# Second FFN product and output projection on 512 columns with four banks of their own, in a hybrid RWKV-7 / S5 block

## The chip, the cores and the metric

The kernel runs on one core of one Trainium2 chip. It is written in a tile language whose scheduler sets the order of the instructions on each engine by a simulated timeline; on the chip each engine then runs its own queue in that order. The metric is the device time of one launch in microseconds.

## What is computed

One layer of a diffusion backbone (2048 latent tokens and 256 context tokens of width 1024, all float32). The reference, cut to what matters:

```python
z = split(modulate(rmsnorm(x, norm1_g), mod[0], mod[1]) @ w_in)      # rwkv columns, gates, S5 columns
rwkv_x = rwkv_mixer(z[:8])    # 3x3 conv, bidirectional delta-rule scan, 8 heads x 64, head norm, gate
s5_x   = s5_mixer(z[8])       # bidirectional diagonal complex scan, 32 groups x 16, then GLU
x = x + mod[2] * (concat([rwkv_x, s5_x]) @ w_out)                    # output projection
h = modulate(rmsnorm(x, norm2_g), mod[3], mod[4])
x = x + mod[5] * ((silu(h @ ffn_w1) * (h @ ffn_w3)) @ ffn_w2)        # ffn_w2: the second FFN product
out = rmsnorm(x, final_g)
```

`modulate(h, shift, scale)` is `h * (1 + scale) + shift`, and the six `mod` vectors come from a small product of the conditioning vector with `mod_w`. The inner FFN width is 2816.

## The kernel before

**Products.** Each large product is made of three matmuls in reduced float32: both operands are split into a high and a low part (`split`: a copy on ScalarE gives the high part, a subtraction on VectorE the low part), and high x high, high x low and low x high are summed in PSUM. PSUM has eight banks of 128 partitions x 512 float32.

**Stages.** `Front` makes the mod vectors, norms and projects the tokens block by block (`project`, L222) and runs the convolutions, in one `f` bank and others of its own. The S5 stage (`s5_pairs`, matmuls L689 to L759, with 32 `mod_group`s beside it) uses three `f` banks of a pool `sf`. The RWKV scan is cut into 36 units of 128 tokens (`R.unit(h)`), which run all through Front, the S5 stage and the start of the last stage. A unit inverts a triangular matrix: 31 serial steps (L999 and L1001, on POOL for most units, on DVE for every second one in the S5 stage), transposes (L1004 to L1008), and two sets of small matmuls (L1014, L1021) that are copied out by ScalarE. Then `chain` runs twice (two chunks of 64 tokens), each a string of small matmuls and copies: L1047, L1052, L1061, L1068 and L1070 on DVE, L1074, L1076, L1082. Heads come in pairs: `par` 0 and 1 are the two halves of the partitions. Matmuls of `par` 0 write to a bank `p0`, those of `par` 1 to a bank `p1`; other banks of this part are `c` and `w`.

**Last stage** (class `Tail`). Four blocks of 512 tokens, in the order 3, 2, 1, 0. For each: `glu` (L1189), `readout` of RWKV (L1209 to L1259), `outproj` (a call of `product`), `norm` (L1340 on POOL makes four scaled identities, L1347 are its 32 matmuls), `ffn` in six parts of 4, 4, 4, 4, 4 and 2 row blocks (w1 and w3 at L1371, 512 tokens at a time; then `product` with w2), and `final`. Block 3's readout, projection, norm and first three FFN parts run beside the last twelve RWKV units and use a pool `fp` of three `f` banks. When the units are done, their pools close, `f2` and a PSUM pool `fq` of three `f` banks open in their place, and `aside(f2, fq)` makes `readout` and `norm` use those; FFN and `product` stay on the three banks of `fp`. From there the loop over b = 3, 2, 1 runs block b's FFN parts between the readout, projection and norm of block b − 1:

```python
early = T.ffn(b, SPLITS[3:5])
for _ in T.readout(b - 1, T.keep):
    next(early, None)
run(early)
T.outproj(b - 1, range(8))
T.norm(b - 1)
run(T.ffn(b, SPLITS[5:]))
```

**`product`** (L1295 to L1303) goes over four column blocks of 256. For each it holds two f banks (two tiles of 128 tokens in each), loads and splits one 128x256 block of weights per row block, runs 4 x 3 matmuls of 256 columns, multiplies by the gate on DVE (L1300, one bank at a time) and adds to the residual on POOL (L1303). On the last call for a block, `square` (L1311, ScalarE) sums the squares for the next norm.

Of the kernel before, what the change touches and what calls it, by code (L numbers as in the profile page):

```python
# [9 lines left out]
F32 = mybir.dt.float32  # L10
F32R = mybir.dt.float32r
# [71 lines left out]

def mod_group(tc, I, K, S, wt, st, fp, n, tag="f"):

    nc = tc.nc
    sec, part = divmod(n, 8)
    mw = I["mod_w"][0].rearrange("(k p) c -> p k c", p=P)
    pm = fp.tile([P, 512], F32, name=tag, bufs=2 if tag == "pa" else None)
# [9 lines left out]
    pc = fp.tile([P, 512], F32, name="f")  # L99
# [20 lines left out]
class Front:  # L120
# [36 lines left out]
    def mods(self):  # L157
        for n in range(16):
            mod_group(self.tc, self.I, self.K, self.S, self.xtile, lambda: self.stile()[:, 0:2 * P], self.fp, n, "pa")
        mod_vectors(self.tc, self.K, 0, (0, 2), "norm1_g", 0)  # L160
        mod_vectors(self.tc, self.K, 0, (1, 3), "norm1_g", 1)
# [621 lines left out]
class Rwkv:  # L783
# [200 lines left out]
    def inverse(self, h, dve):  # L984
# [21 lines left out]
        for q in range(4):  # L1006
            o = 32 * (q % 2)
            nc.vector.transpose(TW[32 * q:32 * q + 32, :, o:o + 32], TN[32 * q:32 * q + 32])  # L1008
        pz = [self.ph.tile([P, 2, 8, 32], F32, name="p%d" % par) for par in range(2)]
        Z = r.tile([P, 8, 32], F32, name="T2")  # L1010
        for b in range(8):
            for par in range(2):
                r0 = 64 * par
                mm(pz[par][r0 + 32:r0 + 64, 0, b, :], AX[1][r0:r0 + 32, :, b], TN[r0:r0 + 32, b, :], start=True, stop=True)  # L1014
        for par in range(2):
            r0 = 64 * par
            act(Z[r0 + 32:r0 + 64], pz[par][r0 + 32:r0 + 64, 0], AF.Copy)
        for b in range(8):
            for par in range(2):
                r0 = 64 * par  # L1020
                mm(pz[par][r0:r0 + 32, 1, b, :], Z[r0 + 32:r0 + 64, b, :], TW[r0 + 32:r0 + 64, b, 32:64], start=True, stop=True)  # L1021
        for par in range(2):
            r0 = 64 * par
            act(TW[r0:r0 + 32, :, 32:64], pz[par][r0:r0 + 32, 1], AF.Copy)

# [10 lines left out]
    def chain(self, h, cc):  # L1036
# [12 lines left out]
        act(R, rs, AF.Copy)  # L1049
        pp = [self.ph.tile([P, 2, 4, 64], F32, name="p%d" % par) for par in range(2)]  # L1050
        for hp, par in every:
            mm(pp[par][RH[par], 0, hp, :], TW[RH[par], cc * 4 + hp, :], R[RH[par], hp, :], start=True, stop=True)  # L1052
        for par in range(2):
            act(UV[RH[par], par], pp[par][RH[par], 0], AF.Copy, scale=-0.5)
        if not last:
# [16 lines left out]
        if h >= 2:  # L1072
            for hp, par in every:
                mm(pp[par][RH[par], 1, hp, :], UV[:, par, hp, :], AR[:, hp, par, :], start=hp == 0, stop=False)  # L1074
            for hp, par in every:
                mm(pp[par][RH[par], 1, hp, :], SV[RH[par], par, hp, :], Q[RH[par], hp, cc, 2, :],  # L1076
                   start=False, stop=hp == 3)
            if cc == 0:
                self.yw = r.tile([P, 4, 128], F32, name="YW")
            cs = slice(64 * cc, 64 * cc + 64)  # L1080
            for par in range(2):
                act(self.yw[RH[par], :, cs], pp[par][RH[par], 1], AF.Copy)  # L1082
# [26 lines left out]
class Tail:  # L1109


    def __init__(self, tc, I, K, S, out, f1, fp):
        self.tc, self.nc, self.I, self.K, self.S, self.out = tc, tc.nc, I, K, S, out
        self.f1, self.fp = f1, fp
        self.side = (f1, fp, "t", "s", "gh", "gl")
        self.C, self.H, self.X = {}, {}, {}
        nc, blk, ident = self.nc, K["blk"], K["ident"]
# [81 lines left out]
    def readout(self, b, put):  # L1199
# [26 lines left out]
        for hf in range(2):  # L1226
# [7 lines left out]
            for hp in range(4):  # L1234
# [175 lines left out]
def hybrid_block(tc, I, out):  # L1410
    with tc.tile_pool(name="dram", bufs=1, space=bass.MemoryType.DRAM) as dp, \
# [4 lines left out]
        with tc.tile_pool(name="a", bufs=1, side="right") as p, \  # L1416
# [11 lines left out]
            for bi in range(5):  # L1428
                if bi < 4:
                    A.block(bi, A.norm(bi + 1))  # L1430
                else:
# [85 lines left out]
```

## Time and profile before

| | us |
|---|---|
| median of 3 runs | 3798.66 |
| lowest and highest run | 3795.69, 3803.98 |
| the profiled execution, its own time | 3793.19 |
| span of its instructions | 3791.4 |

All rows of the trace come from this one profiled execution. Times in them are counted from the start of its span. In the lists of windows, the busy times stand in the order PE (TensorE matmul), PEld (its weight load), DVE (VectorE), ACT (ScalarE), POOL (GpSimd), each followed by its number of instructions. In a timeline a row can stand for several like instructions (x4), and the bracket names the idle time before it and what ended it. A matmul's own length includes its way through the array; the distance of two starts is what it costs when it follows another. Float32 matmuls that are not in the reduced form (those of L755 and L1014, for example) appear as two instructions each.

### The profile page before, as it was taken

Reading aid. Unit: us, or ns where it says so; the run is one execution under the profiler, and the core shown is the slowest. Engines: PE = TensorE matmul, PEld = TensorE weight load, DVE = VectorE, ACT = ScalarE, POOL = GpSimd, SP = SyncE. Lnnn points to the kernel's source line nnn. Section 1 sums busy time; section 2 is a strip of 40 time slices with the busy share of each in tenths; the row PEclk is TensorE's granted clock in tenths of the full one; section 3 lists DMA queues with packets and bytes.
Section 4 is the critical chain, followed back from the end, with each engine's and each line's share of the span. In section 5 each row is a group of like instructions: output and inputs, shape, how many; then the busy total and the mean of one; then the engine's idle time right before and its main releaser. Section 6 shows DMA issues by size and latency. Waiting matters only on the chain. (4 is left out here: it accounts for less than half of the span.)

```text
span 3791.4 us, 70356 instructions
## 1 busy us (share of the span) xinstructions
PE 3375.1 (89%) x25311; PEld 2815.1 (74%) x25311; DVE 2478.8 (65%) x4726; ACT 1710.7 (45%) x3777; POOL 1834.4 (48%) x3184
## 2 busy tenths in 40 slices
PE   5788887888867877889899999999999999999998
PEld 3666666666656666676777888988889888998887
DVE  7768776776778978856766656576444854454444
ACT  3565655645444343354555544454333533343333
POOL 3456667676767666566766662323212321231212
PEclk9798988898767887778889999999999999999999
DMA  6654544454234443276533334454333533333333
GB/s 184 192 138 106 153 120 131 131 141 119 85 105 115 132 142 104 75 168 143 129 90 99 105 98 149 123 164 130 102 98 103 178 101 101 106 100 120 103 100 94
DMA packets 789020, 462.34 MB, mean 122 GB/s; under 512 B 182544, under 2 KB 766868, under 8 KB 788672
## 3 DMA queue, kind: packets, MB, share of 16 engines
q1 hardware_dynamic: 788672, 457.85, 43.5%
q8 instruction: 200, 3.28, 0.4%
q14 instruction: 148, 1.21, 0.1%
HBM read 382.34 MB, written 75.36 MB: 121 GB/s over the span
## 5 line engine op out<-in xcount | busy, mean ns | idle before, releaser
L1303 POOL TENSOR_TENSOR X<-X,t 128x256 f32<-128x256 f32 x464 | 378.1, 842 | 937.3 <-DVE t L1300 936.6
L999 POOL TENSOR_TENSOR tmp<-AT,T 128x60 f32<-128x60 f32 (+24 forms) x992 | 401.2, 404 | 218.6 <-DVE AT L992 109.7
L1144 DVE TENSOR_TENSOR wl<-wr,wh 128x512 fp32r<-128x512 f32 x368 | 264.1, 719 | 312.8 <-PE f L1371 290.2
L1001 POOL TENSOR_TENSOR T<-T,tmp 128x60 f32<-128x60 f32 (+24 forms) x992 | 421.8, 425 | 66.7
L1143 ACT ACTIVATE wh<-wr 128x512 fp32r<-128x512 f32 x368 | 231.9, 631 | 439.9 <-PE f L1371 391.6
L1144 DVE TENSOR_TENSOR vl<-vr,vh 128x256 fp32r<-128x256 f32 x480 | 257.5, 538 | 262.6 <-ACT vh L1143 262.1
L1296 PE MATMUL f<-vl,gh 128*128 128x256 f32 x1408 | 397.2, 289 | 7.7 <-DVE vl L1144 7.5
L1371 PE MATMUL f<-H,wh 128*128 128x512 f32 x1408 | 389.0, 397 | 5.1 <-ACT wh L1143 3.8
L1297 PE MATMUL f<-vh,gl 128*128 128x256 f32 x1408 | 389.9, 284 | 0.0
L1371 PE MATMUL f<-L,wh 128*128 128x512 f32 x1408 | 388.6, 394 | 0.0
L1143 ACT ACTIVATE vh<-vr 128x256 fp32r<-128x256 f32 x480 | 199.2, 416 | 416.4 <-PE f L1297 360.9
L1371 PE MATMUL f<-H,wl 128*128 128x512 f32 x1408 | 386.1, 395 | 0.9 <-DVE wl L1144 0.9
L1295 PE MATMUL f<-vh,gh 128*128 128x256 f32 x1408 | 370.1, 287 | 3.7 <-ACT vh L1143 2.8
L255 DVE SCALAR_TENSOR_TENSOR acc<-zb,cw,acc 128x512 f32<-128x512 f32 (+2 forms) x384 | 307.0, 820 | 23.2 <-ACT acc L251 18.6
L1371 PEld LDWEIGHTS f<-L,wh 128*128 128x128 f32 x1408 | 262.9, 188 | 58.8
L1371 PEld LDWEIGHTS f<-H,wl 128*128 128x128 f32 x1408 | 261.9, 188 | 59.4 <-DVE wl L1144 1.4
L1371 PEld LDWEIGHTS f<-H,wh 128*128 128x128 f32 x1408 | 257.9, 189 | 59.2 <-ACT wh L1143 4.4
L1296 PEld LDWEIGHTS f<-vl,gh 128*128 128x128 f32 x1408 | 269.4, 191 | 18.6 <-DVE vl L1144 12.4
L1297 PEld LDWEIGHTS f<-vh,gl 128*128 128x128 f32 x1408 | 269.6, 192 | 1.2
L1295 PEld LDWEIGHTS f<-vh,gh 128*128 128x128 f32 x1408 | 256.1, 192 | 11.1 <-ACT vh L1143 4.5
L222 PE MATMUL pa<-HI,wl 128*128 128x512 f32 (+1 forms) x712 | 204.8, 407 | 41.4 <-POOL wl L219 30.0
L222 PE MATMUL pa<-HI,wh 128*128 128x512 f32 (+1 forms) x712 | 217.0, 426 | 20.0 <-ACT wh L218 9.7
(458 smaller groups left out, 7501.6 us busy)
## 6 DMA issues: line engine op xcount, KB each, us to landing
wr<-in_ffn_w_dram SPq DMA_DIRECT2D x352, 256.0 KB
raw<-in_w_in_dram SPq DMA_DIRECT2D x178, 256.0 KB
vr<-in_ffn_w_dram SPq DMA_DIRECT2D x352, 128.0 KB
ld<-s_rkvk SPq DMA_DIRECT2D x36, 768.0 KB
mraw<-in_mod_w_dram SPq DMA_DIRECT2D x64, 256.0 KB
vr<-in_w_out_dram SPq DMA_DIRECT2D x128, 128.0 KB
gq<-s_gate SPq DMA_DIRECT2D x116, 128.0 KB
SV<-s_vt SPq DMA_DIRECT2D x144, 64.0 KB
```

Of the source, the lines that this page charges most:

```text
L222: nc.tensor.matmul(pa[:, :nt], w[:, kc, :], h[:, 4 * kh + kc, :nt], start=kh + i + kc == 0, stop=kh == 1 and i == 2 and kc == 3)
L255: nc.vector.scalar_tensor_tensor(ag, zb[:, i0 - 1 + a:i0 - 1 + a + nr, e:e + 64], tap(a, e), ag, op0=OP.mult, op1=OP.add)
L999: eng.tensor_tensor(tv, AT[:, l + 1:, l:l + 1].to_broadcast([P, n, m]), T[:, l:l + 1, 0:m].to_broadcast([P, n, m]), op=OP.mult)
L1001: eng.tensor_tensor(T[:, l + 1:, 0:m], T[:, l + 1:, 0:m], tv, op=OP.add)
L1143: self.nc.scalar.activation(hi, x, AF.Copy)
L1144: self.nc.vector.tensor_tensor(lo, x, hi.bitcast(F32), op=OP.subtract)
L1295: mm(o, ah[:, js], vh, start=k == 0 and j % 2 == 0, stop=False)
L1296: mm(o, ah[:, js], vl, start=False, stop=False)
L1297: mm(o, al[:, js], vh, start=False, stop=k == n - 1 and j % 2 == 1)
L1303: nc.gpsimd.tensor_tensor(x, x, t[:, j], op=OP.add)
L1371: mm(p, a[:, kc, :], h[:, 4 * kh + kc, :], start=kh + i + kc == 0, stop=kh == 1 and i == 2 and kc == 3)
```

## The change

- In the RWKV part, the two tiles `p0` and `p1` become one tile `p`: the two halves of the partitions write to one bank, in the inverse (Z and its follower) and in the chain (U at index 0, y at index 1).
- The bank that this frees goes to `f`: two banks in place of one in `Front`, four in place of three in `sf` and in `fp`.
- When the units are done, a PSUM pool `fo` of four banks `o0` to `o3` opens in place of `fq`. `aside(f2, fo)` leaves `readout` and `norm` on the `f` banks of `fp`, which they now share with FFN's w1 and w3.
- `product` hands over to a new function `wide` once `fo` is set (that is, for all but block 3's projection and its FFN parts [:3]): two column blocks of 512, one bank for each of the four tiles of 128 tokens, weights loaded and split 128x512 at a time in `f2`, DVE's multiply and POOL's add on 128x512. `square` follows with 512 columns.
- The first block's `block(...)` call loses an empty S5 generator.

```diff
-        pz = [self.ph.tile([P, 2, 8, 32], F32, name="p%d" % par) for par in range(2)]
+        pz = self.ph.tile([P, 2, 8, 32], F32, name="p")
...
-                mm(pz[par][r0 + 32:r0 + 64, 0, b, :], AX[1][r0:r0 + 32, :, b], TN[r0:r0 + 32, b, :], start=True, stop=True)
+                mm(pz[r0 + 32:r0 + 64, 0, b, :], AX[1][r0:r0 + 32, :, b], TN[r0:r0 + 32, b, :], start=True, stop=True)
...
-        pp = [self.ph.tile([P, 2, 4, 64], F32, name="p%d" % par) for par in range(2)]
+        pp = self.ph.tile([P, 2, 4, 64], F32, name="p")
...
-        return self.fp.tile([P, 512], F32, name="f")
+        return self.fp.tile([P, 512], F32, name="f", bufs=2)
...
+        self.fo = None
...
-    def aside(self, f2, fq):
+    def aside(self, f2, fo):
-        self.side = (f2, fq, "nt", "ns", "zh", "zl")
+        self.side = (f2, self.fp, "nt", "ns", "zh", "zl")
+        self.fo = fo
...
+    def wide(self, b, A, n, wsrc, grow, last):
+        nc, f1, f2 = self.nc, self.f1, self.side[0]
+        mm = nc.tensor.matmul
+        X1 = self.X[b]
+        for cq in range(2):
+            cols = slice(512 * cq, 512 * cq + 512)
+            gq = f2.tile([P, 512], F32, name="gw", bufs=2)
+            nc.sync.dma_start(gq, bcast_row(grow[cols], 512))
+            po = [self.fo.tile([P, 512], F32, name="o%d" % j) for j in range(4)]
+            for k in range(n):
+                with self.tc.high_priority(offset=1000):
+                    raw = f2.tile([P, 512], F32, name="wr", bufs=3)
+                    nc.sync.dma_start(raw, wsrc(k, cols))
+                    vh = f2.tile([P, 512], F32R, name="wh", bufs=2)
+                    vl = f2.tile([P, 512], F32R, name="wl", bufs=2)
+                    self.split(vh, vl, raw)
+                ah, al = A[k]
+                for j in range(4):
+                    js = slice(j * P, (j + 1) * P)
+                    mm(po[j], ah[:, js], vh, start=k == 0, stop=False)
+                    mm(po[j], ah[:, js], vl, start=False, stop=False)
+                    mm(po[j], al[:, js], vh, start=False, stop=k == n - 1)
+            for j in range(4):
+                t = f1.tile([P, 512], F32, name="t", bufs=2)
+                nc.vector.tensor_tensor(t, po[j], gq, op=OP.mult)
+                x = X1[j][:, cols]
+                nc.gpsimd.tensor_tensor(x, x, t, op=OP.add)
+                if last:
+                    self.square(b, j, cq, t, 512)
...
     def product(self, b, A, n, wsrc, grow, last):
+        if self.fo:
+            return self.wide(b, A, n, wsrc, grow, last)
...
-             tc.tile_pool(name="sf", bufs=3, space=PSUM, side="right") as sf:
+             tc.tile_pool(name="sf", bufs=4, space=PSUM, side="right") as sf:
...
-        with tc.tile_pool(name="f1", bufs=1, side="right") as f1, tc.tile_pool(name="fp", bufs=3, space=PSUM, side="right") as fp:
+        with tc.tile_pool(name="f1", bufs=1, side="right") as f1, tc.tile_pool(name="fp", bufs=4, space=PSUM, side="right") as fp:
...
-            with tc.tile_pool(name="f2", bufs=1) as f2, tc.tile_pool(name="fq", bufs=3, space=PSUM) as fq:
-                T.aside(f2, fq)
+            with tc.tile_pool(name="f2", bufs=1) as f2, tc.tile_pool(name="fo", bufs=1, space=PSUM) as fo:
+                T.aside(f2, fo)
```

Since the scheduler decides, the change also moves instructions that it doesn't name. In the new kernel line numbers after L1113 are higher: FFN's L1371 is L1406, the norm's L1347 is L1382, glu's L1189 is L1191, `wide`'s matmuls are L1295 to L1297, and the old product's are L1330 to L1332. Three places on PE:

**Between the output projection and the norm of block 2** (o_… and f are PSUM banks, `nt` the scaled identity, X the residual rows). Before, with FFN matmuls and those of FFN's product in between:

```order
L1371 MATMUL f<-H,wl 128x512 x4
L1295 MATMUL f<-vh,gh 128x256
L1296 MATMUL f<-vl_27459,gh 128x256
L1297 MATMUL f<-vh,gl 128x256
L1371 MATMUL f<-H,wh 128x512 x4
L1371 MATMUL f<-L,wh 128x512 x4
L1371 MATMUL f<-H,wl 128x512 x4
L1295 MATMUL f<-vh,gh 128x256
L1296 MATMUL f<-vl_27459,gh 128x256
L1347 MATMUL f<-nt,X_26547 128x128
```

Now:

```order
L1296 MATMUL o_26305<-wl,H 128x512
L1297 MATMUL o_26305<-wh,L 128x512
L1296 MATMUL o_26306<-wl,H 128x512
L1297 MATMUL o_26306<-wh,L 128x512
L1296 MATMUL o_26307<-wl,H 128x512
L1297 MATMUL o_26307<-wh,L 128x512
L1382 MATMUL f<-nt,X_26127 128x128 x4
L1382 MATMUL f<-nt,X_26129 128x128 x4
```

The projection's last matmuls (whose weights-side operand is H or L, the split inputs of the projection) now stand right ahead of the norm's, and FFN's L1406 come behind all 32 of these. Blocks 1 and 0 read alike.

**Around the last RWKV unit** (TW and T are the inverse, UV and SV the chain's operands). Before, with FFN matmuls between the unit's groups:

```order
L1371 MATMUL f<-L,wh 128x512 x3
L1371 MATMUL f<-H,wl 128x512 x4
L1371 MATMUL f<-H,wh 128x512 x4
L1371 MATMUL f<-L,wh 128x512 x4
L1371 MATMUL f<-H,wl 128x512 x4
L1052 MATMUL p_22686<-R,TW_1085 64x64 x2
L1052 MATMUL p_22687<-R,TW_1085 64x64 x2
```

Now, the end of the unit before and the start of the last:

```order
L1061 MATMUL c<-UV,BT 64x64 x8
L1074 MATMUL p<-AR,UV 64x64 x8
L1076 MATMUL p<-Q,SV 64x64 x8
L1047 MATMUL c<-SV,Q 64x64 x8
L1014 MATMUL p<-tmp,AY 32x32 x16
L1021 MATMUL p<-TW_1085,T_22529 32x32 x16
L1052 MATMUL p<-R,TW_1085 64x64 x8
```

From the L1014 of the last unit but one to the first readout matmul of block 2, no FFN or product matmul stands in PE's queue. Earlier in this stage the fillers stand some tens of matmuls further ahead of the units than before.

**The end of the S5 matmuls** (L755 and L759). Before, behind the first matmuls of the 23rd unit's chain:

```order
L1061 MATMUL c<-UV,BT 64x64 x2
L759 MATMUL f<-ST,CQ 128x128
L755 MATMUL f<-U,TP 128x128 x2
L759 MATMUL f<-ST,CQ 128x128 x3
L755 MATMUL f<-U,TP 128x128 x2
L759 MATMUL f<-ST,CQ 128x128 x2
L1061 MATMUL c<-UV,BT 64x64 x5
```

Now, ahead of the 21st unit's inverse matmuls:

```order
L759 MATMUL f<-ST,CQ 128x128 x3
L755 MATMUL f<-U,TP 128x128 x2
L759 MATMUL f<-ST,CQ 128x128 x2
L977 MATMUL w<-ident,BK 128x64 x8
L963 MATMUL w<-Q,BK 128x128 x8
L1014 MATMUL p<-tmp,AY 32x32 x16
```

From there to the L1014 of the 24th unit only RWKV matmuls follow; glu's first matmul stands, as before, behind that unit's chain.

## Rows read from the trace of the kernel before

**Rows 1.** The page: busy time, share and instructions of each engine.

```profile
PE 3375.1 (89%) x25311; PEld 2815.1 (74%) x25311; DVE 2478.8 (65%) x4726; ACT 1710.7 (45%) x3777; POOL 1834.4 (48%) x3184
```

**Rows 2.** Windows: busy time by engine, then granted clock, DMA share, GB/s.

```profile
0.00:1060.00 1060.00, 853.56 (x6440) 659.59 (x6440) 764.03 (x1375) 576.46 (x1176) 657.71 (x1172) 0.88 0.50 136
1060.00:1620.00 560.00, 432.38 (x4534) 342.91 (x4531) 475.51 (x954) 225.66 (x554) 374.08 (x631) 0.75 0.40 112
...
1700.00:2044.00 344.00, 313.40 (x2723) 253.81 (x2722) 224.88 (x452) 177.33 (x427) 234.06 (x492) 0.87 0.47 117
...
2290.00:3760.00 1470.00, 1451.29 (x8817) 1285.85 (x8817) 803.43 (x1587) 554.87 (x1216) 361.59 (x447) 1.00 0.40 118
```

**Rows 3.** The page's row of L1296 and two pieces of the chain (start, length).

```profile
L1296 PE MATMUL f<-vl,gh 128*128 128x256 f32 x1408 | 397.2, 289 | 7.7 <-DVE vl L1144 7.5
...
3440.02 0.12 PE f L1297
...
3441.44 2.80 PE f L1371 x12
```

**Rows 4.** Timeline at block 0's norm: start, length, instruction, idle before it.

```profile
3365.41 0.28 PE L1297 MATMUL f<-vh,L 128*128 128x256 f32 x1
...
3365.52 1.28 DVE L1300 TENSOR_TENSOR t<-f,gq 128x512 f32<-128x512 f32 x2
...
3370.76 0.17 DVE L1316 TENSOR_REDUCE ss<-sq 128x4 f32<-128x16 f32 x1 [1.17 <-ACT t L1311]
...
3373.73 1.92 POOL L1340 TENSOR_SCALAR nt<-ident,ss 128x128 f32<-128x128 f32 x4 [3.54 <-DVE ss L77]
...
3377.43 0.83 PE L1347 MATMUL f<-nt,X 128*128 128x128 f32 x6
```

**Rows 5.** Groups of two lines on 128x512: count, busy, mean ns, idle.

```profile
L939 POOL TENSOR_TENSOR BK<-BK,Ei 128x512 f32<-128x512 f32 x36 | 50.3, 1397 | 28.1 <-ACT BK L938 27.8
...
L1143 ACT ACTIVATE wh<-wr 128x512 fp32r<-128x512 f32 x368 | 231.9, 631 | 439.9 <-PE f L1371 391.6
```

**Rows 6.** Windows around a pause of PE in the readout of block 2.

```profile
2325.00:2328.00 3.00, 0.34 (x2) 0.25 (x2) 2.93 (x14) 0.94 (x2) 1.75 (x3) 0.95 0.96 303
2328.00:2335.00 7.00, 6.33 (x29) 5.63 (x29) 5.23 (x14) 3.00 (x7) 1.74 (x2) 0.54 0.32 94
```

**Rows 7.** Timeline of the last two RWKV units, POOL, DVE and PE.

```profile
2181.87 0.53 POOL L999 TENSOR_TENSOR tmp<-AT,T 128x31 f32<-128x31 f32 x1 [5.00 <-PE p L1014]
...
2208.30 0.20 POOL L1001 TENSOR_TENSOR T<-T,tmp 128x8 f32<-128x8 f32 x1
...
2271.41 0.67 DVE L1004 STREAM_TRANSPOSE T<-T 128x256 f32<-128x256 f32 x1 [3.58 <-POOL T L1001]
...
2274.20 1.17 PE L1014 MATMUL p<-tmp,AY 32*32 32x32 f32 x32
```

**Rows 8.** Groups of PE by line, 2218.6 to 2311.9 us.

```profile
L1295 PE MATMUL f<-vh,gh 128*128 128x256 f32 x76 | 21.1, 290 | 0.0
...
L1371 PE MATMUL f<-H,wh 128*128 128x512 f32 x64 | 17.6, 394 | 0.0
```

**Rows 9.** Waits: engine and line, for whom; us in total, times, longest.

```profile
PEld f L94 <- DVE ms L104: 8.8, 4, 5.1
...
PEld f L283 <- DVE acc L284: 8.7, 5, 4.7
```

**Rows 10.** Lines L755, L1189 (first and last start), and L1001 on DVE, 1465 to 1610.

```profile
L755 PE MATMUL f<-U,TP x256: 272/355/583, 1134.6 to 1609.8; 128*128 128x128 f32 x128
...
L1189 PE MATMUL f<-gh,wh x64: 389/496/988, 1641.8 to 1864.4; 128*128 128x512 f32 x64
...
L1001 DVE TENSOR_TENSOR T<-T,tmp 128x60 f32<-128x60 f32 (+24 forms) x31 | 13.2, 425 | 0.6
```

**Rows 11.** Timeline of PE: L1074 by halves, and alternating.

```profile
1255.90 0.63 PE L1074 MATMUL p<-AR,UV 128*64 128x64 f32 x8
...
2215.21 0.64 PE L1074 MATMUL p<-AR,UV 128*64 128x64 f32 x16
```

More of the change, by code (lines that the diff above doesn't have):

```diff
@@ L81, in V, with mod_group @@
     return K["vec"][:, VOFF[n] + i:VOFF[n] + i + 1]
-def mod_group(tc, I, K, S, wt, st, fp, n, tag="f"):
+def mod_group(tc, I, K, S, wt, st, fp, n, tag="f", bufs=None):
     nc = tc.nc
@@ L88, in mod_group @@
     mw = I["mod_w"][0].rearrange("(k p) c -> p k c", p=P)
-    pm = fp.tile([P, 512], F32, name=tag, bufs=2 if tag == "pa" else None)
+    pm = fp.tile([P, 512], F32, name=tag, bufs=bufs)
     w = wt().rearrange("p (k c) -> p k c", k=8)
@@ L98, in mod_group @@
     nc.scalar.activation(rows, pm[:, 0:P], AF.Copy)
-    pc = fp.tile([P, 512], F32, name="f")
+    pc = fp.tile([P, 512], F32, name="f", bufs=bufs)
     if sec in (2, 5):
@@ L158, in mods @@
         for n in range(16):
-            mod_group(self.tc, self.I, self.K, self.S, self.xtile, lambda: self.stile()[:, 0:2 * P], self.fp, n, "pa")
+            mod_group(self.tc, self.I, self.K, self.S, self.xtile, lambda: self.stile()[:, 0:2 * P], self.fp, n, "pa", 2)
         mod_vectors(self.tc, self.K, 0, (0, 2), "norm1_g", 0)
@@ L1013, in inverse @@
                 r0 = 64 * par
-                mm(pz[par][r0 + 32:r0 + 64, 0, b, :], AX[1][r0:r0 + 32, :, b], TN[r0:r0 + 32, b, :], start=True, stop=True)
+                mm(pz[r0 + 32:r0 + 64, 0, b, :], AX[1][r0:r0 + 32, :, b], TN[r0:r0 + 32, b, :], start=True, stop=True)
         for par in range(2):
             r0 = 64 * par
-            act(Z[r0 + 32:r0 + 64], pz[par][r0 + 32:r0 + 64, 0], AF.Copy)
+            act(Z[r0 + 32:r0 + 64], pz[r0 + 32:r0 + 64, 0], AF.Copy)
         for b in range(8):
@@ L1020, in inverse @@
                 r0 = 64 * par
-                mm(pz[par][r0:r0 + 32, 1, b, :], Z[r0 + 32:r0 + 64, b, :], TW[r0 + 32:r0 + 64, b, 32:64], start=True, stop=True)
+                mm(pz[r0:r0 + 32, 1, b, :], Z[r0 + 32:r0 + 64, b, :], TW[r0 + 32:r0 + 64, b, 32:64], start=True, stop=True)
         for par in range(2):
             r0 = 64 * par
-            act(TW[r0:r0 + 32, :, 32:64], pz[par][r0:r0 + 32, 1], AF.Copy)
+            act(TW[r0:r0 + 32, :, 32:64], pz[r0:r0 + 32, 1], AF.Copy)
     def vload(self, h, cc, dst):
@@ L1049, in chain @@
         act(R, rs, AF.Copy)
-        pp = [self.ph.tile([P, 2, 4, 64], F32, name="p%d" % par) for par in range(2)]
+        pp = self.ph.tile([P, 2, 4, 64], F32, name="p")
         for hp, par in every:
-            mm(pp[par][RH[par], 0, hp, :], TW[RH[par], cc * 4 + hp, :], R[RH[par], hp, :], start=True, stop=True)
+            mm(pp[RH[par], 0, hp, :], TW[RH[par], cc * 4 + hp, :], R[RH[par], hp, :], start=True, stop=True)
         for par in range(2):
-            act(UV[RH[par], par], pp[par][RH[par], 0], AF.Copy, scale=-0.5)
+            act(UV[RH[par], par], pp[RH[par], 0], AF.Copy, scale=-0.5)
         if not last:
@@ L1073, in chain @@
             for hp, par in every:
-                mm(pp[par][RH[par], 1, hp, :], UV[:, par, hp, :], AR[:, hp, par, :], start=hp == 0, stop=False)
+                mm(pp[RH[par], 1, hp, :], UV[:, par, hp, :], AR[:, hp, par, :], start=hp == 0, stop=False)
             for hp, par in every:
-                mm(pp[par][RH[par], 1, hp, :], SV[RH[par], par, hp, :], Q[RH[par], hp, cc, 2, :],
+                mm(pp[RH[par], 1, hp, :], SV[RH[par], par, hp, :], Q[RH[par], hp, cc, 2, :],
                    start=False, stop=hp == 3)
@@ L1081, in chain @@
             for par in range(2):
-                act(self.yw[RH[par], :, cs], pp[par][RH[par], 1], AF.Copy)
+                act(self.yw[RH[par], :, cs], pp[RH[par], 1], AF.Copy)
             if cc == 1:
@@ L1305, in product, with square @@
                         self.square(b, 2 * u + j, cq, t[:, j])
-    def square(self, b, j, cq, junk):
+    def square(self, b, j, cq, junk, n=256):
         if (b, "ss") not in self.X:
-            self.X[b, "ss"] = self.f1.tile([P, 4, 4], F32, name="sq", bufs=2)
-        x = self.X[b][j][:, 256 * cq:256 * cq + 256]
+            self.X[b, "ss"] = self.f1.tile([P, 4, 4], F32, name="sq", bufs=2)[:, :, 0:D // n]
+        x = self.X[b][j][:, n * cq:n * cq + n]
         self.nc.scalar.activation(junk, x, AF.Square, accum_out=self.X[b, "ss"][:, j, cq:cq + 1])
@@ L1435, in hybrid_block @@
                     tc.nc.sync.dma_start(DD, S["s5d"])
-                    A.block(bi, s5_pairs(tc, S, K, DD, range(0), [gl], fp), ORDER4, 3)
+                    A.block(bi, order=ORDER4)
                 for d, hs in (((1, (0, 1)), (0, (0, 1))), ((0, (2, 3, 4)),), ((0, (5, 6, 7, 8)),), ((0, (9, 10, 11, 12)),), ())[bi]:
```

## The prediction, made before the changed kernel had run

> **What bounds the kernel now.** I read the page's totals first: TensorE (PE) is busy for 89% of the span and no other engine for more than 65% [rows 1]. That is an average, so I cut the span by stages [rows 2]. Up to 1060 us (Front) PE is busy 854 of 1060 us and VectorE (DVE) 764. From 1060 to 1620 us (the S5 stage) DVE is the fullest, 476 of 560 us. From 2290 us on, PE is busy 1451 of 1470 us at a granted clock of 1.00 (2.4 GHz). There nothing is gained except by fewer PE microseconds, and every wait put in front of PE is paid in full. This last stage holds nearly all of the second FFN product and of the output projection, so the sum is mainly a count of PE time saved and PE idle time made.
>
> **Pace of the products (−17 us).** The page counts 1408 matmuls of 256 columns on a line of the FFN product; in the chain, one that waits for nothing takes 0.120 us, and 12 FFN matmuls of 512 columns take 2.80 us, 0.2333 each [rows 3]. Of the 88 row blocks (22 for each of 4 blocks) the 12 of the parts [:3] of block 3 stay as they were, so 1408 x 3 lines x 76/88 = 3648 change. The output projections of blocks 2, 1 and 0 are 3 x 8 row blocks x 4 column blocks x 4 tiles x 3 = 1152. So 4800 x 0.120 = 576 us become 2400 x 0.2333 = 560 us: −16, and −17 with the hand-overs between column blocks, of which half go. The splits on ScalarE and DVE become half as many and twice as wide, and lie beside the matmuls. By the Trainium skill, "TensorE: Matmul & The Clock Gate", section "Wait — 56ns, not 53.3ns?", a matmul costs its columns at 2.4 GHz and about 2.5 ns more; an estimate from that page would be a gain of 2400 x 2.5 ns = 6 us. The trace shows about 7 ns per matmul saved, and the sum goes by the trace.
>
> **The norm behind the output projection (+36 us).** Before, the norm's matmuls wrote to banks of their own, so FFN matmuls could be put between the last projection matmul and the first norm matmul. The trace shows block 0's: the last projection matmul starts at 3365.41 us, the gate multiply follows, then the adds on GpSimd (POOL) and the squares on ScalarE, the reduction at 3370.76, the reciprocal root, the scaled identity at 3373.73, and the first norm matmul at 3377.43 [rows 4]. PE had FFN matmuls for all of these 12 us. After, norm and FFN take their tiles in program order from one ring of four f banks. The new order shows the projection's last matmul directly followed by the 32 norm matmuls, the FFN behind them, for all of blocks 2, 1 and 0. PE runs in order, so the chain is bare. Its first bank is closed 9 matmuls (2.1 us) before the last. From there: multiply 0.64, four adds of 128x512 on POOL at 1.40 each (the same shape on L939), a last square of 128x512 at 0.63 (ScalarE's split of that shape on L1143 [rows 5]) and 0.2 to read its sum, reduction to scaled identity 2.97, its first quarter 0.48, and 0.5 of handing over: 11 − 2 = 9 us of idle PE. It costs more than itself: after 2325 to 2328, where PE stood for 2.66 us, the granted clock of the next 7 us was 0.54 [rows 6], so about 3 us of work was lost. 9 + 3 = 12 us, three times: +36. Ends: 6 us each if the adds and the rsqrt run faster with nothing beside them (+18), 16 if other POOL and DVE work queues in between (+48).
>
> **The end of the RWKV chain (+20 us).** The last units' inverse is a serial loop on POOL: it starts when the unit before has run its first inverse matmuls and goes from 2181.87 to 2208.50 us without a break, 26.6 us; transposes take from 2271.41 to the matmul at 2274.20 in the last unit, 2.8 us [rows 7]; then come steps of 0.7 to 0.9 us one behind the other (that row's x32 takes 1.17); I count 17 of them, an estimate of 15 us with hand-over, and 3 us for the readout's first operand. Together some 48 us. Before, PE had FFN and product matmuls between these units: 64 on each of three lines and 76 on each of three from 2218.6 to 2311.9 [rows 8], 192 x 0.233 + 228 x 0.120 = 72 us, more than the hole. In the new order none is left there: from the first inverse matmuls of the last unit but one, only RWKV matmuls stand in the queue, since block 3's later FFN parts now share the f ring with the readout and are ordered behind it. Of 48 us some 18 are RWKV's own PE work; 30 stay idle, with 7 more just before and 3 of slow clock: 40. Against it, the same filler runs earlier, among the former units, where PE lacked 31 of 344 us (1700 to 2044 in [rows 2]) and was at 0.87 of its clock; I let half of the 40 come back: +20. Ends: 0 and +50.
>
> **The freed bank in Front and S5 (−5 us).** PE's weight load waited 8.7 us for DVE to read an f bank at L283 in Front, and 8.8 us at L94 in the S5 stage [rows 9]. With two banks for one I take −5 us, ends −25 and +5. The S5 stage's order changes most: its last matmul lay between the inverse matmuls of the 23rd and 24th unit, and now stands before the 21st's, so three units run bare behind it. It started at 1609.8, and the first matmul behind the stage (glu, L1189) at 1641.8. After, the S5 work ends earlier by what 2.7 units take of DVE: every second unit has its inverse there, 24 us (L1001, 13.2, and L999 beside it [rows 10]), and some 17 more are in each; 2.7 x 29 / 0.88 = 89 us. Against that, three bare units of 25 to 40 us (two inverses can run at once, on POOL and on DVE) and 17 us stand where 32 us stood: +60 to +105. It balances, so 0, with ends −45 and +40.
>
> **Left at nothing:** the column blocks' hand-over in a product (bank 0 is read while the other three banks' last matmuls run; without that, 0.7 us in each of 30), the U and y tiles in one bank (priced as a rival), and the end of the kernel behind the last matmul (the same adds and squares, ±3).
>
> **Sum:** −17 + 36 + 20 − 5 = +34 us on the profiled execution of 3793.19 us gives 3827. The median of the runs stands 5.5 us above that execution, so 3832 us.
>
> **Rivals.**
> (a) *Faster: the freed bank shortens the first 1620 us.* DVE stands still for 296 us in Front and 84 in the S5 stage [rows 2]. If PE's waits for banks are what spaces DVE's work, the 17 us of [rows 9] and half of S5's 84 go: −60 in place of −5, 3777 us. It decides as soon as more than 39 us are gained there. For it: with four banks the S5 work is drawn together by three units. Against it: DVE is already at 85% in S5, most of what it waits for isn't PE, and the order of Front by units hardly moves.
> (b) *Slower still: two row halves in one bank run one behind the other.* L1014, L1021, L1052 and L1076 use the two halves of PE's rows in turn; before, these wrote to two banks. Where eight passes of one half were grouped, 8 took 0.63 us on L1074, as long as 16 that alternate, 0.64 [rows 11]. If alternation stopped helping, each of seven groups of a unit (L1014 counting double, L1052 and L1076 twice) would cost about 0.55 us more: 12 units x 7 x 0.55 = 46 us where PE is the bound, 3878 us. No row of before has this pattern in one bank, so nothing excludes it; against it, the two halves write to different partitions, and PE's work per unit is small before 1700 us. The Trainium skill speaks for it, "TensorEngine Tiling (Array Packing)", "Gotcha 1: PSUM Pressure": "Different row tiles cannot access same PSUM bank simultaneously"; no run so far shows whether it holds here.
> (c) *No change:* the early filler repays the RWKV end in full, and the bare norm costs 6 us without loss of clock: −17 + 18 − 5 = −4, 3795 us.
>
> **How the numbers follow.** My forecast gets 0.60 (its own range is 3800 to 3865, by the ends of the norm and of the RWKV end), (a) 0.20, (b) 0.10, (c) 0.10. Less than 0.2%, about 7.6 us, can't be told from no change here. So faster 0.20, same 0.10, slower 0.70. The range, 3770 to 3880, leaves out the far half of (a) and of (b).
>
> **What would show it.** In the profile after: product matmuls at 0.233 us each; three PE gaps of about 9 us ahead of the norm's matmuls, released by POOL's scaled identity and each followed by a stretch of granted clock near half; 30 us or so of idle PE around the last two RWKV units, on POOL's inverse; the last S5 matmul near 1520 us, and glu's first still near 1640. If the readout of block 2 begins before 2290 us, the first stages gained and (a) holds; if L1052's 16 passes take 1.2 us, (b). I am wrong at the root if PE is busy in the norm gaps.

## Result: slower by 1.0%, close to the forecast

The changed kernel takes 3837.74 us (median of 6 runs, 3831.31 to 3843.51) against 3796.83 us before (6 runs on the same chip): a ratio of 1.0102, interval [1.0087, 1.0118]. In a later set of runs the ratio was 1.0095 [1.0075, 1.0116]. The forecast was 3832 us in a range of 3770 to 3880.

The profiled execution of the changed kernel has a span of 3829.6 us, 38.2 us more than before. Its windows, in the same order of columns as [rows 2] (stages end where they end in this trace):

```profile
0.00:1060.00 1060.00, 851.92 (x6475) 657.06 (x6475) 784.69 (x1393) 582.96 (x1194) 658.77 (x1181) 0.88 0.50 137
1060.00:1545.00 485.00, 356.71 (x3704) 278.07 (x3705) 412.52 (x802) 176.83 (x432) 336.73 (x521) 0.74 0.42 119
1545.00:1644.00 99.00, 70.59 (x979) 58.98 (x979) 59.50 (x161) 51.50 (x126) 39.48 (x104) 0.63 0.28 71
1644.00:2044.00 400.00, 353.21 (x3077) 281.91 (x3073) 275.47 (x516) 220.08 (x507) 279.16 (x563) 0.91 0.52 132
2044.00:2165.00 121.00, 116.93 (x1056) 96.87 (x1055) 75.52 (x124) 73.03 (x148) 80.85 (x179) 0.97 0.36 105
2165.00:2289.00 124.00, 83.83 (x1083) 71.53 (x1081) 55.44 (x101) 47.61 (x119) 66.71 (x176) 0.83 0.21 61
2289.00:3800.00 1511.00, 1470.00 (x6509) 1191.30 (x6509) 789.46 (x1404) 515.03 (x931) 319.44 (x263) 0.99 0.39 117
```

Front is as before. The S5 stage ends earlier, and the stretch from there to glu is wide, with PE's clock at 0.63 and DVE busy for 60 of 99 us. From 2165 to 2289 us, around the last two RWKV units, PE is busy 84 of 124 us. The last stage, which before had 19 us of PE idle in 1470, now has 41 in 1511. The last S5 matmul and the first of glu (first and last start, as in [rows 10]):

```profile
L755 PE MATMUL f<-U,TP x256: 272/275/583, 1107.4 to 1545.7; 128*128 128x128 f32 x128
...
L1191 PE MATMUL f<-gh,wh x64: 387/397/988, 1644.2 to 1843.0; 128*128 128x512 f32 x64
```

S5 is done 64 us earlier than before, glu starts 2.4 us later: earlier S5 and three bare units balance.

What PE waited for in the last part, from 2200 us to the last matmul: us in total, times, and the longest. After, the three largest:

```profile
PE f L1382 <- POOL nt L1375: 27.9, 3, 9.3
PE p L1014 <- ACT tmp L1005: 24.5, 2, 13.3
PE f L1215 <- ACT rh L1145: 5.1, 1, 5.1
```

and the two largest of before:

```profile
PE f L1296 <- DVE vl L1144: 4.8, 11, 0.8
PE f L1371 <- ACT wh L1143: 3.8, 4, 1.6
```

The three rows of after are the two holes that the prediction priced: three times 9.3 us ahead of the norm, and 13.3 + 11.2 + 5.1 us around the last two RWKV units. The first one of the norm's, in the timeline (compare [rows 4]):

```profile
2485.20 0.39 PE L1297 MATMUL o<-wh,L 128*128 128x512 f32 x1
...
2485.62 1.29 DVE L1300 TENSOR_TENSOR t<-o,gw 128x512 f32<-128x512 f32 x2
...
2486.39 2.50 POOL L1302 TENSOR_TENSOR X<-X,t 128x512 f32<-128x512 f32 x2 [16.43 <-DVE t L1300]
2486.55 0.39 PE L1297 MATMUL o<-wh,L 128*128 128x512 f32 x1
...
2487.64 1.79 DVE L1146 TENSOR_TENSOR wl<-wr,wh 128x512 fp32r<-128x512 f32 x1 [0.73 <-ACT wh L1145]
...
2488.24 0.19 ACT L1346 ACTIVATION_READ_ACCUMULATOR t<-X 128x1 f32 x1
...
2489.36 1.28 DVE L1300 TENSOR_TENSOR t<-o,gw 128x512 f32<-128x512 f32 x2
...
2490.12 2.49 POOL L1302 TENSOR_TENSOR X<-X,t 128x512 f32<-128x512 f32 x2 [1.23 <-DVE t L1300]
...
2493.39 0.16 DVE L1351 TENSOR_REDUCE ss<-sq 128x4 f32<-128x8 f32 x1 [2.76 <-ACT t L1346]
...
2495.83 1.43 POOL L1375 TENSOR_SCALAR nt<-ident,ss 128x128 f32<-128x128 f32 x4 [3.23 <-DVE ss L77]
2496.26 4.00 PE L1382 MATMUL f<-nt,X 128*128 128x128 f32 x17 [9.32 <-POOL nt L1375]
```

The last projection matmul starts at 2486.55, the first norm matmul at 2496.26, and PE does nothing between. One link was not in the forecast: POOL stands for 1.23 us between its second and third add, until the third gate multiply (2489.36) is done. That multiply needs a buffer `t`, which exists twice, so it comes behind the first square; but that one had been read out at 2488.43. What it stood behind after that is a split in DVE's queue (2487.64) that took 1.79 us beside POOL's adds, where one of the same shape took 0.69 us at 2484.93.

**Where the 38 us are.** Summing for each kind of matmul the time from its start to the next start on PE, from the first readout matmul of block 2 to the last matmul, gives 1462.9 us before and 1522.6 after. Part by part: FFN 802.6 to 852.7, because 192 matmuls (44.8 us) that ran ahead of the readout now run behind it, and 5.3 us more, 3.5 of them between 2290 and 2320 us, just behind the RWKV end, where the clock starts at 0.58; products and projections 595.2 to 568.4 without the norm's gaps, although 60 (7.2 us, in 256 columns) more of them lie here; the gaps 0 to 27.9; the norm's own 192 matmuls 19.9 to 34.7; the readout's 45.0 to 38.8. The stretch ahead of it, from glu to that readout, fell from 670.8 to 644.4 us, but has lost 52 us of that FFN and product work, so the RWKV end cost 26 net. Up to glu it is 2.4 us more, and 2.4 behind the last matmul: 2.4 − 26.4 + 59.7 + 2.4 = 38.1.

### The profile page after: what moved, and what is told of

Its sections match the earlier page's. It is cut to its first block, busy times and chain, and to the rows that moved or that the text cites. A ratio compares the mean times of both kernels' runs of the same rounds, so it can differ in the third digit from the quotient of the medians.

```text
span 3829.6 us, 64049 instructions
## 1 busy us (share of the span) xinstructions
PE 3314.2 (87%) x22911; PEld 2643.2 (69%) x22911; DVE 2468.7 (64%) x4526; ACT 1674.6 (44%) x3475; POOL 1791.7 (47%) x2992
## 3 DMA queue, kind: packets, MB, share of 16 engines
q14 instruction: 137, 1.12, 0.1%
## 4 chain that ended last, share of the span: by engine, by line
PE 50%; POOL 18%; DVE 14%; issue 6%; DMA 4%; ACT 4%; SPq 1%; POOLq 0%; DVEq 0%; ACTq 0%
PE f L1406 23%; POOL T L1001 7%; POOL tmp L999 6%; PE o L1295 5%; PE o L1296 4%; PE o L1297 4%; PE pa L222 4%; PE w L963 2%; DVE acc L255 1%; POOL wl L219 1%; DVE ST L746 1%; ACT AX L970 1%; DMA yl<-s_y 1%; DVE Q L947 1%; DVE T L1001 1%
## 5 line engine op out<-in xcount | busy, mean ns | idle before, releaser
L1146 DVE TENSOR_TENSOR wl<-wr,wh 128x512 fp32r<-128x512 f32 x568 | 449.5, 796 | 451.4 <-ACT wh L1145 220.4
L1145 ACT ACTIVATE wh<-wr 128x512 fp32r<-128x512 f32 x568 | 357.3, 632 | 835.1 <-PE f L1406 451.8
L1302 POOL TENSOR_TENSOR X<-X,t 128x512 f32<-128x512 f32 x192 | 272.6, 1442 | 813.2 <-DVE t L1300 804.2
L1001 POOL TENSOR_TENSOR T<-T,tmp 128x60 f32<-128x60 f32 (+24 forms) x992 | 412.3, 416 | 67.4
L1406 PE MATMUL f<-H,wh 128*128 128x512 f32 x1408 | 390.9, 397 | 10.4 <-ACT wh L1145 5.2
L1406 PE MATMUL f<-H,wl 128*128 128x512 f32 x1408 | 391.2, 396 | 5.0 <-DVE wl L1146 4.9
L1406 PE MATMUL f<-L,wh 128*128 128x512 f32 x1408 | 388.9, 395 | 0.0
L1406 PEld LDWEIGHTS f<-H,wh 128*128 128x128 f32 x1408 | 261.3, 188 | 71.5 <-ACT wh L1145 6.3
L1406 PEld LDWEIGHTS f<-H,wl 128*128 128x128 f32 x1408 | 263.6, 189 | 67.1 <-DVE wl L1146 7.2
L1406 PEld LDWEIGHTS f<-L,wh 128*128 128x128 f32 x1408 | 264.5, 189 | 60.7
L1296 PE MATMUL o<-wl,gh 128*128 128x512 f32 x608 | 240.5, 396 | 0.0
L1295 PE MATMUL o<-wh,gh 128*128 128x512 f32 x608 | 228.0, 399 | 3.2 <-DVE t L1300 2.5
L1297 PE MATMUL o<-wh,gl 128*128 128x512 f32 x608 | 229.6, 395 | 0.0
L222 PE MATMUL pa<-LO,wh 128*128 128x512 f32 (+1 forms) x712 | 206.2, 409 | 3.3 <-DVE LO L202 3.3
L222 PEld LDWEIGHTS pa<-HI,wl 128*128 128x128 f32 x712 | 135.8, 209 | 98.4 <-POOL wl L219 48.8
L1300 DVE TENSOR_TENSOR t<-o,gw 128x512 f32<-128x512 f32 x192 | 129.1, 686 | 110.3 <-PE o L1297 76.5
L222 PEld LDWEIGHTS pa<-HI,wh 128*128 128x128 f32 x712 | 139.5, 215 | 48.7 <-ACT wh L218 15.0
```

Of the source, the lines that this page charges most:

```text
L222: nc.tensor.matmul(pa[:, :nt], w[:, kc, :], h[:, 4 * kh + kc, :nt], start=kh + i + kc == 0, stop=kh == 1 and i == 2 and kc == 3)
L1001: eng.tensor_tensor(T[:, l + 1:, 0:m], T[:, l + 1:, 0:m], tv, op=OP.add)
L1145: self.nc.scalar.activation(hi, x, AF.Copy)
L1146: self.nc.vector.tensor_tensor(lo, x, hi.bitcast(F32), op=OP.subtract)
L1295: mm(po[j], ah[:, js], vh, start=k == 0, stop=False)
L1296: mm(po[j], ah[:, js], vl, start=False, stop=False)
```

## The experiments

All ratios are to the kernel before, run beside the kernel on the same chip. 0.1% is 3.8 us.

**1. Only the banks.** One bank p, the freed bank to f; product, readout and norm as before.

```diff
-        self.side = (f2, self.fp, "nt", "ns", "zh", "zl")
-        self.fo = fo
+        self.side = (f2, fq, "nt", "ns", "zh", "zl")
...
-            with tc.tile_pool(name="f2", bufs=1) as f2, tc.tile_pool(name="fo", bufs=1, space=PSUM) as fo:
-                T.aside(f2, fo)
+            with tc.tile_pool(name="f2", bufs=1) as f2, tc.tile_pool(name="fq", bufs=3, space=PSUM) as fq:
+                T.aside(f2, fq)
```

> The kernel before with the RWKV part on one bank p and the freed bank given to f (Front 2, S5 stage 4, last stage 4), but the product on 256 columns and readout and norm on three banks of their own, as before. Theory (bank sharing in the RWKV part costs nothing, Front and S5 gain or lose a few us, norm and RWKV end are covered as before): 3797 with -10 to +5, that is 3787 to 3802 us, L1052's 16 passes at 0.69 us. Rival (the regrouped S5 stage with its three bare units, or the row halves in one bank, are what costs the time): 3815 us or more.

Measured: 1.0000 [0.9986, 1.0013], 3801.89 us beside 3802.65. L1052, two row halves in one bank p:

```profile
2205.64 0.68 PE L1052 MATMUL p<-R,TW 64*64 64x64 f32 x16
```

16 passes in 0.68 us; in two banks, in the trace of before, they took 0.68 to 0.69. In both traces they start in pairs, 7 ns apart, and a pair follows the last by 58 ns in most cases. Rival (b) falls, and so does (a): the whole S5 regrouping is in this kernel (its last S5 matmul is at 1551 us, glu at 1650), and it neither gains nor costs.

**2. The FFN part ahead of the norm.**

```diff
+                    run(T.ffn(b, SPLITS[5:]))
                     T.norm(b - 1)
-                    run(T.ffn(b, SPLITS[5:]))
```

> The changed kernel with one line moved: block b's last FFN part stands ahead of the norm of block b - 1 in the program, so that its product (48 matmuls of 512 columns, 11.2 us) lies between the projection's last matmul and the norm's first, three times. Theory (the bare norm costs some 12 us, three times): the three gaps of 9.3 us of the changed kernel vanish, and the time falls by 30 to 36 us, to 3802 to 3808 us. Rival (the gap is only moved: what hides the norm is missing behind it, since the FFN part is then gone there): within 10 us of the changed kernel, 3828 to 3838.

Measured: 1.0055 [1.0039, 1.0072], some 18 us below the changed kernel, half of what was expected. The three gaps shrank from 9.3 to 2.8 us, not to nothing, although 11.2 us of products lay in them: the chain itself had become longer. DVE's queue in this kernel, from the reduction through the reciprocal root, with POOL's adds:

```profile
2515.49 0.14 DVE L1351 TENSOR_REDUCE ss<-sq 128x4 f32<-128x8 f32 x1
...
2515.71 1.68 POOL L1302 TENSOR_TENSOR X<-X,t 128x512 f32<-128x512 f32 x1 [1.29 <-DVE ss L1351]
...
2516.16 1.26 DVE L1352 TENSOR_SCALAR ss<-ss 128x4 f32<-128x4 f32 x1
...
2517.34 0.68 DVE L1300 TENSOR_TENSOR t<-o,gw 128x512 f32<-128x512 f32 x1
...
2518.16 1.30 POOL L1302 TENSOR_TENSOR X<-X,t 128x512 f32<-128x512 f32 x1 [0.76 <-DVE va L70]
...
2518.32 1.15 DVE L73 TENSOR_TENSOR va<-va,va 128x4 f32<-128x4 f32 x1
...
2519.59 0.69 DVE L1300 TENSOR_TENSOR t<-o,gw 128x512 f32<-128x512 f32 x1
...
2520.42 1.28 POOL L1302 TENSOR_TENSOR X<-X,t 128x512 f32<-128x512 f32 x1 [0.97 <-DVE va L72]
...
2520.58 1.15 DVE L75 SCALAR_TENSOR_TENSOR va<-va,va 128x4 f32<-128x4 f32 x1
...
2521.87 0.69 DVE L1300 TENSOR_TENSOR t<-o,gw 128x512 f32<-128x512 f32 x1
```

From the reduction on, the root that took 2.4 us bare takes 7.3. Three gate multiplies of the FFN product (0.7 us each) stand between its steps, and three steps that took 0.16 to 0.17 us bare took 1.15 to 1.26 us. Each of these ends within 0.03 us of the end of one of POOL's adds. Over the whole trace, 36 steps of such roots (L1352, L70 to L77) took more than 0.6 us, and all 36 began while a POOL instruction ran; none of the 324 that began with POOL idle did (48 that began beside a POOL instruction stayed short). So the root is held up beside POOL's adds, and more adds lie beside it now; a multiply that waits there for a free `t` does not show.

**3. A bank of its own for the norm.** `fp` with three banks, the norm's tiles on a pool `fn` of one.

```diff
...
-            pt = self.ftile(None, fq)
+            pt = self.ftile(None, self.fn)
...
```

> The changed kernel with the norm's matmuls on one bank of their own and three f banks in place of four, so that norm and FFN don't share a ring. Theory (the shared ring is what puts the FFN behind the norm): the scheduler finds cover again, the three gaps vanish as with the moved line, and the time is 3800 to 3812 us; the end of the RWKV chain stays bare. Rival (the order comes from the four o banks or from the 512-column product, not from the ring): the gaps stay, 3830 to 3845 us.

Measured: 1.0171 [1.0156, 1.0186], slower than the changed kernel and outside both ranges. The gap did shrink, from 9.3 to 3.2 us, with FFN product matmuls ahead of it again, but behind it the norm's eight tiles follow each other on the one bank:

```profile
2540.92 1.64 PE L1382 MATMUL f<-nt,X 128*128 128x128 f32 x8 [3.23 <-POOL nt L1375]
2543.47 2.08 PE L1382 MATMUL f<-nt,X 128*128 128x128 f32 x8 [0.90 <-DVE ns L1384]
2545.19 0.77 PE L1406 MATMUL f<-H,wh 128*128 128x512 f32 x1
2546.45 2.08 PE L1382 MATMUL f<-nt,X 128*128 128x128 f32 x8 [0.48 <-DVE ns L1384]
```

The norm takes 24 to 26 us in place of 10 to 11, with FFN matmuls in between. So the ring does put the FFN behind the norm, but taking a bank out of it for the norm costs more than it brings: summed from start to start as above, the FFN takes 878 us (853 in the changed kernel) and the readout 52 (39), against 12 us less for the products with their gaps. Three f banks serve readout and FFN here; that this is the reason was not shown apart.

**4 and 5. Work for the RWKV end.** Two, and then one, of block 3's FFN parts ahead of the end of the chain. The one:

```diff
-            run(T.ffn(3, SPLITS[:3]))
+            run(T.ffn(3, SPLITS[:4]))
...
-                    early = T.ffn(b, SPLITS[3:5])
+                    early = T.ffn(b, SPLITS[3 + b // 3:5])
```

> The changed kernel with block 3's FFN parts [3:5] moved ahead of the end of the RWKV chain, where the kernel before had them in effect; 8 of its row blocks go back to 256 columns (+1.3 us). Theory (the bare end of the chain costs about 20 us): 3813 to 3822 us, the gaps of 13.3 and 11.2 us ahead of the last two units' first inverse matmuls covered by FFN matmuls, readout of block 2 later by some 25 us. Rival (the hole is the price of work already done earlier and the filler only moves): 3832 to 3840 us.

> The changed kernel with only one more FFN part of block 3 (4 row blocks: 96 FFN matmuls and 192 product matmuls of 256 columns, some 45 us of PE work) ahead of the end of the RWKV chain; one part stays beside block 2's readout. Theory (the bare end holds some 30 us of idle PE, and taking two parts away bared the readout instead): 12 to 22 us below the changed kernel, a ratio of 1.004 to 1.007 to the kernel before. Rival (nothing but the 12 us that two parts gave is to be had, since the filler is missing later): 1.007 to 1.010.

One part holds 192 FFN matmuls, not the 96 of the expectation, and 192 x 0.233 + 192 x 0.120 = 68 us of PE work. Measured: with two parts 1.0070 [1.0053, 1.0087], some 12 us below the changed kernel and between the two theories; with one 1.0016 [1.0006, 1.0027]. In both, the waits of L1014 on the inverse are gone. With two parts, block 2's readout and projection have no FFN beside them: PE is busy 80 of 107 us there at a clock of 0.81 (2393 to 2500 us); 9.3 of the 27 idle us are the norm's gap. With one part the gain is 30 to 33 us (against 1.0095 and 1.0102), more than either theory gave, and about as much as the hole's three waits, 13.3 + 11.2 + 5.1 us.

**6. The width undone.** The new product on its four banks, but 256 columns at a time.

```diff
-        for cq in range(2):
-            cols = slice(512 * cq, 512 * cq + 512)
+        for cq in range(4):
+            cols = slice(256 * cq, 256 * cq + 256)
...
```

> The changed kernel with the new product on 256 columns (four column blocks, the same four banks o0 to o3, half of each used), so that banks, rings and the bare norm stay and only the width is undone. Theory of the prediction (0.120 against 0.1167 per 256 columns: 17 us): 17 to 20 us slower than the changed kernel, a ratio of 1.0145 to 1.0155 to the kernel before. Second theory, from the sums of start-to-start times in the last stage (a 256-column matmul with its waits 0.1256, a half of one of 512 columns 0.1185): 27 to 34 us, 1.017 to 1.019. Rival (2.5 ns per matmul saved, and the rest hidden): 6 us, 1.012.

> The changed kernel with its new product on 256 columns, once more and beside it. Theory from the traces (the width is worth 17 to 19 us of PE, but 3 x 2.5 us of it come back because the adds behind the last column block, and so the bare gap ahead of the norm, are shorter): 8 to 14 us slower than the changed kernel run beside it, 0.2 to 0.4%. Rival one (the width is worth nothing): within 4 us of it. Rival two (the prediction's term stands undiminished): 16 us or more slower.

And the changed kernel beside the second of these:

> The changed kernel once more, so that it stands beside the 256-column form on the same chip: a ratio of 1.009 to 1.012 to the kernel before by both theories.

Measured: 1.0102 [1.0081, 1.0123] the first time, below all that was expected and not to be told from the changed kernel's first ratio; the second time 1.0134 [1.0113, 1.0154] beside 1.0095 [1.0075, 1.0116] for the changed kernel on the same chip. Medians 10.6 us apart, ratios 0.39%: 11 to 15 us. In the traces, from the first readout matmul of block 2 to the last matmul, the products take 593.5 us in place of 568.4 (the norm's gaps taken out). That is 25.1 more, of which 4.8 are PE's idle time between them. But the norm's wait is shorter:

```profile
PE f L1382 <- POOL nt L1375: 20.2, 3, 6.8
```

27.9 − 20.2 = 7.7 us come back, since the last adds (0.72 us in place of 1.25) and squares (0.42 in place of 0.63) of a column block are shorter. The readout takes 3.5 us less and the end behind the last matmul 2.1; why the readout does was not followed.

**7. Both repairs.** Experiment 2 with a last part of three row blocks and a third buffer for the gated rows (`wt`; the gate row `gw` keeps one buffer in place of two), alone and with the one part of experiment 5.

```diff
-SPLITS = [(0, 4), (4, 8), (8, 12), (12, 16), (16, 20), (20, 22)]
+SPLITS = [(0, 4), (4, 8), (8, 12), (12, 16), (16, 19), (19, 22)]
...
-            gq = f2.tile([P, 512], F32, name="gw", bufs=2)
+            gq = f2.tile([P, 512], F32, name="gw")
...
-                t = f1.tile([P, 512], F32, name="t", bufs=2)
+                t = f1.tile([P, 512], F32, name="t", bufs=2) if j % 2 else f2.tile([P, 512], F32, name="wt")
```

> The moved line again (FFN's last part ahead of the norm), with three row blocks in that part in place of two and a third buffer for the gated rows, since in the first run of it the chain to the norm had grown from 11 to 19 us: the gate multiplies of the FFN part waited for their buffer in front of the rsqrt's steps on VectorE. Theory: the gap of 3.0 us and the starved products ahead of it go, 9 to 15 us below that run, a ratio of 1.0015 to 1.003. Rival (the slow norm is bound by VectorE's order, not by the buffers): 1.004 to 1.006.

> Both repairs together. Theory (norm and RWKV end are separate costs, and add up): the sum of the two gains, a ratio of 0.996 to 1.000 to the kernel before. Rival (they fill with the same work, which then is missing in one place): no better than the moved line alone, 1.002 to 1.005.

> The kernel with both repairs once more: 0.991 to 0.994 of the kernel before.

> Both repairs, the new product on 256 columns. Here the norm is covered, so no shorter gap gives anything back. Theory (width is 17 to 19 us of PE where PE is the bound): 14 to 20 us slower than the repaired kernel beside it, a ratio of 0.996 to 0.998 to the kernel before. Rival (the gain over the kernel before is one of banks and order, and the width is worth nothing): within 5 us of it.

Measured: the norm's repair alone 1.0045 [1.0026, 1.0064], where 1.0015 to 1.003 was expected. That is in the rival's range, and within the intervals it is no better than experiment 2 (1.0055). The wait for the scaled identity is gone from its trace, but waits in the middle of the norm's matmuls have come in its place, so more cover and more buffers move the wait and DVE's queue goes on holding the norm:

```profile
PE f L1382 <- DVE ns L1384: 12.1, 3, 4.0
```

Both together give 0.9925 [0.9909, 0.9942], where 0.996 to 1.000 was expected, and, on another chip, 0.9946 [0.9928, 0.9963], 3779 us. This is 0.5 to 0.75% below the kernel before. What PE waits for with both, from 2200 us on, the largest two:

```profile
PE f L1382 <- DVE ns L1384: 8.1, 2, 4.0
PE o L1295 <- ACT wh L1145: 3.3, 5, 0.8
```

Two norms still have such a wait of 4.0 us. At block 1's (2935.8 to 2941.8 us) three of the FFN product's multiplies and three splits stand in DVE's queue ahead of the copy that frees the norm's bank, and beside POOL's adds the splits take 1.15 to 1.75 us. The same on 256 columns gives 0.9960 [0.9946, 0.9973], 7 us slower by the medians and 5 by the ratios, where 14 to 20 were expected by the theory and at most 5 by the rival. From the first readout matmul of block 2 to the last matmul the products take 576.7 us against 551.5, so the width is worth 25 us of PE here too, 10 of them idle time; but the norm's 192 matmuls take 20.2 us against 32.6, and the FFN 807.7 against 816.9. Why these are shorter was not followed. On PE the width's gain shows in both pairs, and it is mostly handed back by other stages.

## Why the prediction was right, point by point

- **What bounds it.** Right. The waits made in front of PE in the last stage showed up in the time, and the kernel with both holes filled runs below the kernel before.
- **Pace, −17 us.** Right in sign, undersized. The width gave 25.1 and 25.2 us in two pairs of traces; without PE's idle time between the products it gave 20.3 and 15.2, which is the term as it was set. Waits inside the products were set to nothing. Some 9 us more came beside the width: products and projections cost 595.2 us for 4740 matmuls before, which is 603 for 4800, and 593.5 for 4800 of the same width on the four banks of their own. Of these 9 us, 5.4 are idle time that before lay ahead of readout matmuls behind a product matmul; the rest was not followed.
- **The bare norm, +36 us.** Right in mechanism, with the gap at 9.3 us for a forecast of 9. That it fits so well is partly luck: the first bank closes 6 matmuls before the last one (2485.20 and 2486.55, 1.4 us), not 9, and POOL's wait of 1.2 us was not foreseen; but the adds took 1.25 us and not 1.40, reduction to scaled identity 2.4 and not 3.0, and the hand-over to PE 0.4 in place of 1.0. Behind the gap the term was undersized: the norm's own matmuls grew by 14.8 us, more than the 3 x 3 us set for the clock. That makes 27.9 + 14.8 = 43, inside the upper end given. The clock after the gap, and PE's waits at the end of the norm:

```profile
2486.80:2496.20 9.40, 0.14 (x1) 0.77 0.26 80
2496.20:2503.00 6.80, 6.74 (x35) 0.56 0.00 0
2503.00:2508.00 5.00, 3.76 (x32) 1.00 0.00 0
...
2505.49 2.05 PE L1382 MATMUL f<-nt,X 128*128 128x128 f32 x16 [0.78 <-DVE ns L1384]
2508.32 1.19 PE L1406 MATMUL f<-H,wh 128*128 128x512 f32 x4 [0.78 <-DVE ns L1384]
```

  PE works 6.8 us at 0.56 of its clock, which costs the 3 us that were set; not set were the two waits of 0.78 us for DVE to empty the norm's banks.
- **The RWKV end, +20 us.** Right in mechanism: from 2231.0 to 2288.6 us PE is idle for 36 us, where 37 was set, 13.3, 11.2 and 5.1 of them in three waits; and 12 us of its work ran at a clock of 0.50, some 6 us lost. Undersized was the net cost, by the step that let half of it come back because filler runs earlier: of these 42 us the accounting leaves 26, and filling the hole gained 30 to 33, so 9 to 16 came back where 20 was set.

```profile
2243.64 1.20 PE L1014 MATMUL p<-tmp,AY 32*32 32x32 f32 x32 [13.33 <-ACT tmp L1005]
...
2247.68 1.12 PE L1052 MATMUL p<-R,TW 64*64 64x64 f32 x16 [0.85 <-ACT TW L1024]
...
2253.98 0.68 PE L1052 MATMUL p<-R,TW 64*64 64x64 f32 x16 [0.48 <-ACT R L1049]
...
2270.10 1.20 PE L1014 MATMUL p<-tmp,AY 32*32 32x32 f32 x32 [11.16 <-ACT tmp L1005]
...
2288.68 0.94 PE L1215 MATMUL f<-rh,ER 128*128 128x256 f32 x2 [5.06 <-ACT rh L1145]
```

  The first L1052 row, 1.12 us, comes near the 1.2 us that was to speak for rival (b); but the granted clock is 0.50 there, and the same 16 passes take 0.68 us at 2253.98.

- **Front and S5, −5 and 0.** No gain shows: +2.4 us to glu in this trace (+2 to +14 in the traces of all the experiments, against the one trace of before), and the bank change alone measured 1.0000. Both lie within the ends given. The last S5 matmul was set near 1520 us and came at 1546, which cost nothing.
- **Left at nothing.** The column blocks' hand-over held: L1295 waits 2.5 us in all for it. The end of the kernel grew by 2.4 us, inside ±3.
- **The test for rival (a)** was badly put: block 2's readout does begin before 2290 us (2288.7), but because 52 us of work had been moved behind it, not because the first stages gained.
- So the direction and the three large terms were right, each undersized: 2 up to glu, −34 for the products, 43 for the norm, 26 for the RWKV end and 5 in the FFN, most of it just behind that, −6 for the readout and 2 at the end make 38. That the sum came within 4 us of +34 is luck: products and readout gave 17 and 6 us more than was set, and norm, RWKV end, FFN, Front and the end took 7, 6, 5, 7 and 2 more.

## What to carry to other kernels

Giving two stages one ring of buffers gave them one order here: what is late in the program could no longer run ahead and cover the other's latency, and on the engine that bounds the kernel an uncovered chain is paid for (here 9.3 us, three times), and again in clock behind it (3 us each). When a change reorganises banks, read in the new order what stands in the bounding engine's queue behind each serial chain before counting the pace of the changed loop. A wider operation saves little per element here (about 5 ns for each matmul of 256 columns, idle time included), and makes the last step of the chain behind it longer; here filling the two holes (two pieces of filler moved, and one more buffer) was worth 1.5 to 1.8%, the width 0.1 to 0.4%.

## What the runs showed of the hardware

- Two halves of PE's rows writing to one PSUM bank cost nothing that shows: 16 passes of L1052 take 0.68 us in one bank as in two, starting in pairs 7 ns apart in both, and the kernel that differs in this and the f banks runs at 1.0000. "Different row tiles cannot access same PSUM bank simultaneously", says the Trainium skill ("TensorEngine Tiling (Array Packing)", "Gotcha 1: PSUM Pressure"); if they take turns here, it does not lengthen these groups.
- Idle PE is paid a second time: after 12.6 us without a matmul the granted clock was 0.50 (1.2 GHz) for the next 8.4 us of RWKV work, and 16 passes of L1052 took 1.12 us there, 0.68 us later in the same unit.

```profile
2231.00:2243.60 12.60, 0.00 (x0) 0.56 0.00 0
2243.60:2252.00 8.40, 6.11 (x120) 0.50 0.01 2
2252.00:2258.50 6.50, 4.80 (x104) 0.92 0.16 50
```

- Steps on DVE can be held up beside POOL's adds: steps on 128x4 that take 0.16 us bare took 1.15 to 1.26 us in experiment 2, each ending with the add that ran beside it, and in the changed kernel a split of 128x512 took 1.79 us in place of 0.69. The chain over DVE was longer where filler brought more adds beside it.
